# Strassen's left operands made one by one, the residual spread, and single PSUM banks in the last block

## The chip, the cores and the metric

The kernel runs on one core of a Trainium2 chip. The metric is the device time of one execution in microseconds (us), the median of three runs. The program is one launch with no arithmetic on the host.

## The reference

One layer of a transformer block on a sequence of 512 tokens with width 2048, all in float32. The part that the change touches is the second half:

```python
x = layer_norm(alpha * x + gate1 * mix, ln1_g, ln1_b)
u2 = x * (1.0 + scale2) + shift2
h = jnp.square(jax.nn.relu(u2 @ w_mlp_up)) @ w_mlp_down      # 2048 -> 8192 -> 2048
x = layer_norm(alpha * x + gate2 * h, ln2_g, ln2_b)
```

Before it come two attention branches and their projections, which the change leaves as they are.

## The kernel before

Every float32 operand of a large product is split into a rounded high part and a low part (`whi` and `wlo` for weights): ScalarE copies the high part out, VectorE subtracts it from the original to get the low part. One product is then three matmuls into the same PSUM bank (lines 206 to 208). Line 208 of the up projection, and line 207 of the down products, are the ones that read `wlo`.

The 8192 hidden columns are worked in 16 blocks of 512. Blocks 0 to 12 use Strassen's seven products for the down projection. For block `fb` the kernel merges two lists of steps:

- the up projection of block `fb`: eight steps, called U0 to U7 below. A step loads two 128-row weight tiles, splits them, and does 24 matmuls of 512 columns. After U7 the relu (ScalarE) and the multiplication (VectorE) write the tiles `rA` and `rB`, first `rA` from the first PSUM pair, then `rB`.
- the down products of block `fb - 1`: fourteen steps, the seven products in the order 1, 5, 2, 7, 6, 3, 4 for each of two column halves. They are called P1, P5 and so on, with a dash (P1') in the second half. A step loads or combines weight tiles (`draw`, five buffers), splits them, does 12 matmuls of 512 columns into a PSUM pair and adds that to an accumulator (line 1177; in the first Strassen block ScalarE copies it instead, line 1175).

Each product needs a left operand (`sh`, `sl`), made from `rA` and `rB` by `s_ops`: a split on ScalarE and VectorE for each of the seven, and four more VectorE operations of the same size that combine quarters (lines 1109, 1110, 1114, 1118). In the kernel before, an object `Ahead` makes them: as soon as the last up step has been written down, every left operand whose buffer the previous block has used for the last time is made, and the rest follow as their buffers come free. In program order they stand ahead of P3', P4' and of U0 of the next block.

The order of instructions on each engine isn't the program order: a planner walks through the program with its own cost estimates and gives each engine, whenever it is free, the earliest instruction in program order that is ready by then. Each engine then runs its list strictly in that order. So program order is a priority.

`residual(cb)` (lines 1058 to 1070) scales and shifts one 512-column block of the residual by `ln1_g` and `ln1_b`: two loads on POOL's queue, two multiplications on ScalarE, four VectorE operations of 1024 elements, two stores to DRAM (`x_d`) on POOL's queue. All four run beside the second half of the up projection of block 0, `mlp_up(0, 1)`. After it the PSUM pool is closed and a new one with pairs of banks (tags `u` and `d`) is opened.

The last block (lines 1308 to 1339) goes by four token tiles t and four column groups g: 12 matmuls into half of a PSUM pair (`ed`), an add into the residual, statistics. After the four groups the tile is normalised: ScalarE scales, then a multiplication and an addition by POOL (t = 0, 1, and g = 0 of t = 2) or VectorE (the other groups of t = 2); t = 3 is finished by VectorE alone, with two fused operations for each group.

Of the kernel before, what the change touches and what calls it, by code (L numbers as in the profile page):

```python
# [84 lines left out]
def tile_block(  # L85
# [182 lines left out]
    def merge(*lists, lo=0.0, hi=1.0):  # L268
        order = []
        for n, l in enumerate(lists):  # L270
            b0, b1 = (lo, hi) if n else (0.0, 1.0)
            order += [(b0 + (i + 0.5) / len(l) * (b1 - b0), n, i) for i in range(len(l))]
        order.sort()
        for _, n, i in order:
            lists[n][i]()
# [551 lines left out]
    def advance(force=False):  # L827
        nonlocal step_no
        step_no += 1
        while pend and (pend[0][0] <= step_no or force):  # L830
            pend.pop(0)[1]()
# [196 lines left out]
    def mlp_up(fb, half=None, r=None):  # L1028
        r = [] if r is None else r
        ts_ = slice(0, S) if half is None else slice(half * 256, half * 256 + 256)  # L1030
        hold = {}

        def mk():
            hold["d"] = [pair(f"u{fb}_{j}", "u") for j in range(2)]
            return [d[:, j] for d in hold["d"] for j in range(2)]

        def done(banks):
            if not r:
                r.extend(hp.tile([P, 2, S], F32, name=n, tag=n, bufs=1) for n in ("rA", "rB"))
            if half is None:  # L1040
                for rt, d in zip(r, hold["d"]):
                    nc.scalar.activation(rt, d, AF.Relu)
                    nc.vector.tensor_mul(rt, rt, d)
            else:
                for j in range(4):
                    rt = r[j // 2][:, j % 2, ts_]
                    nc.scalar.activation(rt, banks[j][:, ts_], AF.Relu)
                    nc.vector.tensor_mul(rt, rt, banks[j][:, ts_])  # L1048

        return r, group_fm(  # L1050
            w_mlp_up[0], fb * 512, 512, u2, all_k, f"u{fb}_{half}", done, ps, ts_, wload2,
            mk if half is None else None,
        )
# [3 lines left out]

    def residual(cb):
        cs = slice(cb * 512, (cb + 1) * 512)
        g1t = opp["p"].tile([P, 512], F32, name=f"g1t{cb}", tag="g1t", bufs=2)  # L1060
        b1t = opp["p"].tile([P, 512], F32, name=f"b1t{cb}", tag="b1t", bufs=2)
        nc.gpsimd.dma_start(g1t, ln1_g[0:1, cs].broadcast_to([P, 512]))
        nc.gpsimd.dma_start(b1t, ln1_b[0:1, cs].broadcast_to([P, 512]))
        nc.scalar.mul(g1t, g1t, ALPHA)
        nc.scalar.mul(b1t, b1t, ALPHA)
        for h_ in range(2):
            rc = res2[h_][:, :, cs]
            nc.vector.tensor_mul(rc, rc, g1t.unsqueeze(1).broadcast_to([P, 2, 512]))
            nc.vector.tensor_add(rc, rc, b1t.unsqueeze(1).broadcast_to([P, 2, 512]))
            nc.gpsimd.dma_start(x_d[h_][cb].rearrange("p (t c) -> p t c", t=2), rc)  # L1070
# [1 line left out]

    r_new, steps = mlp_up(0, 0)
    merge(steps, u2_steps(1), lo=0.1, hi=0.9)
    merge(mlp_up(0, 1, r_new)[1], [lambda c_=c_: residual(c_) for c_ in range(4)])
    st_o.close()
    st_ps.close()
    psd["p"], st_ps = pool("ps3", space=PSUM)
    ctx.callback(st_ps.close)

# [2 lines left out]

    sp, st_sp = pool("strassen")
    ORD = (1, 5, 2, 7, 6, 3, 4)

    def s_tiles(i):
# [29 lines left out]
        return [(1, lambda: split(1, a11)), (5, m5), (2, lambda: split(2, a12)), (7, lambda: split(7, a11)),  # L1121
                (6, m6), (3, m3), (4, lambda: split(4, a22))]

    class Ahead:
        def __init__(self):
            self.todo, self.free = [], set(ORD)

        def advance(self):
            while self.todo and self.todo[0][0] in self.free:
                i, fn = self.todo.pop(0)  # L1130
                self.free.discard(i)
                fn()

    ahead = Ahead()

    def strassen(fb, ops):
        st = {}

        def step(cg, i):
            def raw(j, k):  # L1140
                return wraw(
                    w_mlp_down[0][fb * 512 + (j - 1) * 256 : fb * 512 + j * 256, (k - 1) * 1024 + cg * 512 : (k - 1) * 1024 + cg * 512 + 512],
                    sp, "draw", 5,
                )

            if i == 1:
                w = st["b11"] = raw(1, 1)
            elif i == 5:
                st["b12"] = raw(1, 2)
                w = st["b11"]  # L1150
                nc.vector.tensor_sub(w, st["b12"], w)
            elif i == 2:
                w = st["b21"] = raw(2, 1)
            elif i == 7:
                st["b22"] = raw(2, 2)
                w = st["b12"]
                nc.vector.tensor_sub(w, st["b22"], w)
            elif i == 6:
                w = st["b11"]
                nc.vector.tensor_sub(w, st["b22"], w)  # L1160
            elif i == 3:
                w = st["b22"]
            else:
                w = st["b11"]
                nc.vector.tensor_sub(w, w, st["b21"])
            wh, wl = parts(w)
            db = pair(f"p{fb}_{cg}_{i}", "d")
            sh, sl = ops[i]
            for t in range(2):
                ts_ = slice(t * P, (t + 1) * P)  # L1170
                for k in range(2):
                    mm3(db[:, t], sh[:, k, ts_], sl[:, k, ts_], wh[k], wl[k], k == 0, k == 1)
            ac = acc[i][:, :, cg * 512 : cg * 512 + 512]
            if fb == 0:
                nc.scalar.copy(ac, db)
            else:
                nc.vector.tensor_add(ac, ac, db)  # L1177
            if cg == 1:
                ahead.free.add(i)
            ahead.advance()  # L1180

        return [lambda cg=cg, i=i: step(cg, i) for cg in range(2) for i in ORD]

    ops = {}
    ahead.todo = s_ops(r_new, ops)
    ahead.advance()
    for fb in range(1, NSB + 1):
        r_new, steps = mlp_up(fb)
        nxt = {}

        def begin(r_new=r_new, nxt=nxt, fb=fb):
            if fb < NSB:
                ahead.todo = s_ops(r_new, nxt)
                ahead.advance()

        last_up = steps.pop()

        def last_step(last_up=last_up, begin=begin):
            last_up()
            begin()  # L1200

        steps.append(last_step)
        merge(steps, strassen(fb - 1, ops), lo=0.1, hi=1.1)
        ops = nxt


    def load_g2b(tiles):
# [97 lines left out]
    lw, st_lw = pool("lastw", side="right")  # L1305
    merge(down_steps(NFB - 2, prev), [lambda g=g, k0=k0: last_w(lw, g, k0) for g in range(4) for k0 in (0, 2)], lo=0.2, hi=1.0)
    prev = cur
    for t in range(NT):
        st = ep.tile([P, 4, 6], F32, name=f"st2_{t}")
        rt = res[t]  # L1310
        for g in range(4):
            cs = slice(g * 512, (g + 1) * 512)
            if g % 2 == 0:
                ed = pair(f"e{t}_{g}", "du"[g // 2])
            bk = ed[:, g % 2]
            for k in range(4):
                wh, wl = lwt[g, k // 2 * 2]
                ts_ = slice(t * P, (t + 1) * P)
                mm3(bk, prev[k][0][:, ts_], prev[k][1][:, ts_], wh[k % 2], wl[k % 2], k == 0, k == 3)
            nc.vector.tensor_add(rt[:, cs], rt[:, cs], bk)  # L1320
            nc.vector.bn_stats(st[:, g, :], rt[:, cs])
        mv = ep.tile([P, 2], F32, name=f"mv2_{t}")
        nc.vector.bn_aggr(mv, st)
        ve = ep.tile([P, 1], F32, name=f"ve2_{t}")
        nc.vector.tensor_scalar_add(ve, mv[:, 1:2], LN_EPS)
        y = rstd(ep, ve, 1, f"n2{t}")
        nm = ep.tile([P, 1], F32, name=f"nm2_{t}")
        nc.vector.scalar_tensor_tensor(nm, mv[:, 0:1], -1.0, y, ALU.mult, ALU.mult)
        for g in range(4):
            cs = slice(g * 512, (g + 1) * 512)  # L1330
            if t < NT - 1:
                nc.scalar.activation(rt[:, cs], rt[:, cs], AF.Identity, bias=nm, scale=y)
                eng = nc.gpsimd if t < 2 or g == 0 else nc.vector
                eng.tensor_mul(rt[:, cs], rt[:, cs], g2t[:, cs])
                eng.tensor_add(rt[:, cs], rt[:, cs], b2t[:, cs])
            else:
                nc.vector.scalar_tensor_tensor(rt[:, cs], rt[:, cs], mv[:, 0:1], g2t[:, cs], ALU.subtract, ALU.mult)
                nc.vector.scalar_tensor_tensor(rt[:, cs], rt[:, cs], y, b2t[:, cs], ALU.mult, ALU.add)
            nc.sync.dma_start(out[0][t * P : (t + 1) * P, cs], rt[:, cs])
    st_lw.close()  # L1340
    st_e.close()
    st_dp.close()
# [28 lines left out]
```

## Time and profile before

| | |
|---|---|
| median of three runs | 2807.77 us (2805.59 to 2807.94) |
| the profiled execution | 2807.5 us, of which its span 2805.7 us |
| mean granted TensorE clock | 0.98 of full speed |
| busy: TensorE, VectorE, ScalarE, POOL | 96%, 68%, 37%, 7% of the span |

The numbered groups further down quote the trace. A row of a timeline has the start in us from the span's start, the length in us, the engine (PE is TensorE, DVE VectorE, ACT ScalarE), the line, the operation and what it writes and reads; in brackets stands the idle time just before it, with what ended it. A row of a waits view has the total in us, the number of waits and the longest. Rows that overlap are normal on PE, where matmuls are pipelined: the distance from one start to the next is what one costs.

### The profile page before, as it was taken

Reading aid. Unit: us, or ns where it says so; the run is one execution under the profiler, and the core shown is the slowest. Engines: PE = TensorE matmul, PEld = TensorE weight load, DVE = VectorE, ACT = ScalarE, POOL = GpSimd, SP = SyncE. Lnnn points to the kernel's source line nnn. Section 1 sums busy time; section 2 is a strip of 40 time slices with the busy share of each in tenths; the row PEclk is TensorE's granted clock in tenths of the full one; section 3 lists DMA queues with packets and bytes.
Section 4 is the critical chain, followed back from the end, with each engine's and each line's share of the span. In section 5 each row is a group of like instructions: output and inputs, shape, how many; then the busy total and the mean of one; then the engine's idle time right before and its main releaser. Section 6 shows DMA issues by size and latency. Waiting matters only on the chain.

```text
span 2805.7 us, 33125 instructions
## 1 busy us (share of the span) xinstructions
PE 2699.3 (96%) x12456; PEld 2233.2 (80%) x12456; DVE 1915.9 (68%) x2761; ACT 1030.9 (37%) x1668; POOL 189.3 (7%) x236
## 2 busy tenths in 40 slices
PE   7999999999999999999999999999999999999997
PEld 6888998888777777787888778777877778778885
DVE  6984347655588877537866776776666776679575
ACT  4433242222377642224644332333323333333231
POOL 0212000000122211100000000000000000000003
PEclk9999999999999999999999999999999999999998
DMA  8773339877511157535653233322323233235331
GB/s 295 263 237 91 98 120 310 277 262 234 194 50 42 61 182 250 194 128 177 194 196 112 76 105 98 98 93 88 105 90 98 90 98 106 83 105 188 98 128 60
DMA packets 217100, 404.94 MB, mean 144 GB/s; under 512 B 18334, under 2 KB 45124, under 8 KB 216172
## 3 DMA queue, kind: packets, MB, share of 16 engines
q1 hardware_dynamic: 207824, 370.61, 40.6%
q0 software_dynamic: 8928, 32.14, 3.4%
q8 instruction: 98, 1.61, 0.2%
q14 instruction: 62, 0.51, 0.1%
q10 hardware_dynamic: 188, 0.07, 0.0%
HBM read 385.94 MB, written 16.83 MB: 144 GB/s over the span
## 4 chain that ended last, share of the span: by engine, by line
PE 50%; DVE 8%; DMA 2%; issue 1%; ACT 1%; POOL 0%; DVEq 0%; ACTq 0%; POOLq 0%
PE u L208 8%; PE u L206 7%; PE u L207 7%; PE p L208 5%; PE p L207 5%; PE p L206 5%; PE o L207 2%; PE o L208 2%; PE o L206 2%; DVE sl L1106 1%; DVE res L1177 1%; DVE wlo L1013 1%; PE bb L208 1%; PE bb L206 1%; PE bb L207 1%
## 5 line engine op out<-in xcount | busy, mean ns | idle before, releaser
L199 ACT CAST whi<-raw 128x512 fp32r<-128x512 f32 (+4 forms) x456 | 269.9, 597 | 565.7 <-PE g L207 204.6
L208 PE MATMUL u<-u2h,wlo 128*128 128x512 f32 (+1 forms) x1088 | 423.1, 392 | 51.5 <-DVE wlo L1013 51.4
L200 DVE TENSOR_TENSOR wlo<-raw,whi 128x512 fp32r<-128x512 f32 (+4 forms) x456 | 301.8, 674 | 244.2 <-ACT whi L199 242.8
L206 PE MATMUL u<-u2h,whi 128*128 128x512 f32 (+1 forms) x1088 | 420.3, 387 | 2.2 <-DVE rB L1048 2.2
L207 PE MATMUL u<-u2l,whi 128*128 128x512 f32 (+1 forms) x1088 | 419.5, 386 | 0.0
L348 DVE SCALAR_TENSOR_TENSOR acc<-araw,csil,acc 128x512 f32<-128x512 f32 (+1 forms) x382 | 279.2, 749 | 83.9 <-DMA araw<-in_w_ada_dram 78.9
L1012 ACT CAST whi<-draw 128x1024 fp32r<-128x1024 f32 x182 | 191.9, 1055 | 382.6 <-PE p L208 235.1
L1013 DVE TENSOR_TENSOR wlo<-raw,whi 128x1024 fp32r<-128x1024 f32 x152 | 185.5, 1221 | 186.4 <-ACT whi L1012 186.2
L1012 ACT CAST whi<-raw 128x1024 fp32r<-128x1024 f32 x152 | 159.7, 1051 | 393.4 <-PE u L207 319.5
L1013 DVE TENSOR_TENSOR wlo<-draw,whi 128x1024 fp32r<-128x1024 f32 x182 | 221.9, 1220 | 100.2 <-ACT whi L1012 100.2
L208 PEld LDWEIGHTS u<-u2h,wlo 128*128 128x128 f32 x1088 | 212.9, 196 | 96.2 <-DVE wlo L1013 56.5
L207 PE MATMUL p<-wlo,sh 128*128 128x512 f32 x728 | 283.2, 389 | 0.0
L208 PE MATMUL p<-whi,sl 128*128 128x512 f32 x728 | 283.2, 389 | 0.0
L206 PE MATMUL p<-whi,sh 128*128 128x512 f32 x728 | 283.2, 389 | 0.0
L206 PEld LDWEIGHTS u<-u2h,whi 128*128 128x128 f32 x1088 | 212.4, 195 | 41.6 <-DVE rB L1048 2.4
L207 PEld LDWEIGHTS u<-u2l,whi 128*128 128x128 f32 x1088 | 211.2, 194 | 40.1
L206 PE MATMUL g<-uh,whi 128*128 128x512 f32 x512 | 201.3, 393 | 0.0
L208 PE MATMUL g<-uh,wlo 128*128 128x512 f32 x512 | 200.3, 391 | 0.0
L207 PE MATMUL g<-ul,whi 128*128 128x512 f32 x512 | 200.1, 391 | 0.0
L207 PEld LDWEIGHTS p<-wlo,sh 128*128 128x128 f32 x728 | 136.7, 188 | 28.5
L206 PEld LDWEIGHTS p<-whi,sh 128*128 128x128 f32 x728 | 136.7, 188 | 28.4
L208 PEld LDWEIGHTS p<-whi,sl 128*128 128x128 f32 x728 | 136.6, 188 | 28.2
(379 smaller groups left out, 4891.4 us busy)
## 6 DMA issues: line engine op xcount, KB each, us to landing
araw<-in_w_ada_dram SPq DMA_DIRECT2D x192, 512.0 KB, 5.0
raw<-in_w_mlp_up_dram SPq DMA_DIRECT2D x136, 512.0 KB, 3.7
draw<-in_w_mlp_down_dram SPq DMA_DIRECT2D x104, 512.0 KB, 3.4
raw<-in_w_in_dram SPq DMA_DIRECT2D x96, 512.0 KB, 5.1
raw<-in_w_out_dram SPq DMA_DIRECT2D x48, 512.0 KB, 3.5
raw<-in_w_mlp_down_dram SPq DMA_DIRECT2D x24, 512.0 KB, 3.4
gate_d<-sg POOLq DMA_DIRECT2D x32, 256.0 KB, 5.8
raw<-in_w_branch_fox_dram SPq DMA_DIRECT2D x16, 512.0 KB, 4.9
```

Of the source, the lines that this page charges most:

```text
L199: nc.scalar.copy(hi, rv[:, k])
L200: nc.vector.tensor_sub(lo, rv[:, k], f(hi))
L206: nc.tensor.matmul(o, ah, bh, start=start, stop=False)
L207: nc.tensor.matmul(o, ah, bl, start=False, stop=False)
L208: nc.tensor.matmul(o, al, bh, start=False, stop=stop)
L348: nc.vector.scalar_tensor_tensor(ac, rv[:, kk, :], ck_, ac, ALU.mult, ALU.add)
L1012: nc.scalar.copy(hi, raw)
L1013: nc.vector.tensor_sub(lo, raw, f(hi))
L1106: nc.vector.tensor_sub(lo, a, f(hi))
L1177: nc.vector.tensor_add(ac, ac, db)
```

## The change

- `residual` takes one tile of the `draw` buffers for both vectors instead of two of its own, and ScalarE scales both in one instruction. Residuals 0 and 2 stay beside `mlp_up(0, 1)`, at 0.55 and 1.05 of its length; residuals 1 and 3 move into the first Strassen block, between P6 and P3 and between P3 and P4. The pool of the Strassen tiles is opened earlier for that.
- `Ahead` goes. At the start of each block the left operand of product 1 is made, that of product 5 after U0, and each product step then makes one more, two products ahead. The fourteen product steps and the one for operand 5 are spread over the same length as before, so U0 and U1 now stand together ahead of P1.
- Before the last block the PSUM pool is closed and one with eight single banks is opened.
- For t = 2, POOL finishes groups 0 to 2. Group 3 stays with VectorE and is put off until the statistics of group 2 of t = 3 have been written down.

```diff
     def residual(cb):
         cs = slice(cb * 512, (cb + 1) * 512)
-        g1t = opp["p"].tile([P, 512], F32, name=f"g1t{cb}", tag="g1t", bufs=2)
-        b1t = opp["p"].tile([P, 512], F32, name=f"b1t{cb}", tag="b1t", bufs=2)
+        gb = sp.tile([P, 2, 512], F32, name="draw", tag="draw", bufs=5)
+        g1t, b1t = gb[:, 0], gb[:, 1]
         nc.gpsimd.dma_start(g1t, ln1_g[0:1, cs].broadcast_to([P, 512]))
         nc.gpsimd.dma_start(b1t, ln1_b[0:1, cs].broadcast_to([P, 512]))
-        nc.scalar.mul(g1t, g1t, ALPHA)
-        nc.scalar.mul(b1t, b1t, ALPHA)
+        nc.scalar.mul(gb, gb, ALPHA)
...
-    merge(mlp_up(0, 1, r_new)[1], [lambda c_=c_: residual(c_) for c_ in range(4)])
     st_o.close()
+    sp, st_sp = pool("strassen")
+    merge(mlp_up(0, 1, r_new)[1], [lambda c_=c_: residual(c_) for c_ in (0, 2)], lo=0.3, hi=1.3)
     st_ps.close()
     psd["p"], st_ps = pool("ps3", space=PSUM)
...
-            if cg == 1:
-                ahead.free.add(i)
-            ahead.advance()
+
+            if lefts:
+                lefts.pop(0)[1]()
...
     for fb in range(1, NSB + 1):
+        ops = {}
+        lefts = s_ops(r_new, ops)
         r_new, steps = mlp_up(fb)
-        nxt = {}
-
-        def begin(r_new=r_new, nxt=nxt, fb=fb):
-            if fb < NSB:
-                ahead.todo = s_ops(r_new, nxt)
-                ahead.advance()
...
-        merge(steps, strassen(fb - 1, ops), lo=0.1, hi=1.1)
-        ops = nxt
+        first, second = lefts.pop(0)[1], lefts.pop(0)[1]
+        down = strassen(fb - 1, ops, lefts)
+        if fb == 1:
+            down.insert(6, lambda: residual(3))
+            down.insert(5, lambda: residual(1))
+        first()
+        down.insert(0, second)
+        merge(steps, down, lo=0.1, hi=1.1)
...
+    st_ps.close()
+    ps, st_ps = pool("ps4", space=PSUM)
+    ctx.callback(st_ps.close)
+    late = []
     for t in range(NT):
...
-            if g % 2 == 0:
-                ed = pair(f"e{t}_{g}", "du"[g // 2])
-            bk = ed[:, g % 2]
+            bk = bank(f"e{t}_{g}", "e", 8, ps)
...
             nc.vector.bn_stats(st[:, g, :], rt[:, cs])
+            if g == 2:
+                while late:
+                    late.pop()()
...
-                eng = nc.gpsimd if t < 2 or g == 0 else nc.vector
-                eng.tensor_mul(rt[:, cs], rt[:, cs], g2t[:, cs])
-                eng.tensor_add(rt[:, cs], rt[:, cs], b2t[:, cs])
+
+                def finish(eng, t=t, rt=rt, cs=cs):
+                    eng.tensor_mul(rt[:, cs], rt[:, cs], g2t[:, cs])
+                    eng.tensor_add(rt[:, cs], rt[:, cs], b2t[:, cs])
+                    nc.sync.dma_start(out[0][t * P : (t + 1) * P, cs], rt[:, cs])
+
+                if t < 2 or g < 3:
+                    finish(nc.gpsimd)
+                else:
+                    late.append(lambda finish=finish: finish(nc.vector))
```

## Rows read from the trace of the kernel before

**Rows 1.** the page of the profile: span, and busy time of each engine

```profile
span 2805.7 us, 33125 instructions
...
PE 2699.3 (96%) x12456; PEld 2233.2 (80%) x12456; DVE 1915.9 (68%) x2761; ACT 1030.9 (37%) x1668; POOL 189.3 (7%) x236
```

**Rows 2.** waits of TensorE over the whole span: total us, times, longest

```profile
PE u L208 <- DVE wlo L1013: 51.4, 12, 4.5
```

**Rows 3.** waits of TensorE, blocks from 1590 to 2485 us

```profile
PE u L208 <- DVE wlo L1013: 49.8, 11, 4.5
```

**Rows 4.** timeline of TensorE, one block's end, and the last such end

```profile
1574.76 0.39 PE L208 MATMUL p<-whi,sl 128*128 128x512 f32 x1
...
1589.04 0.39 PE L208 MATMUL p<-whi,sl 128*128 128x512 f32 x1
...
1590.17 0.39 PE L206 MATMUL p<-whi,sh 128*128 128x512 f32 x1
1595.09 0.79 PE L208 MATMUL u<-u2h,wlo 128*128 128x512 f32 x1 [4.53 <-DVE wlo L1013]
...
1597.38 0.63 PE L206 MATMUL u<-u2h,whi 128*128 128x512 f32 x1
...
1599.09 0.62 PE L207 MATMUL u<-u2l,whi 128*128 128x512 f32 x1
...
2482.04 0.80 PE L208 MATMUL u<-u2h,wlo 128*128 128x512 f32 x1 [4.53 <-DVE wlo L1013]
```

**Rows 5.** timeline of VectorE at the same block's end

```profile
1584.27 0.69 DVE L1106 TENSOR_TENSOR sl<-rA,sh 128x512 fp32r<-128x512 f32 x1 [0.69 <-ACT sh L1105]
...
1585.61 1.21 DVE L1043 TENSOR_TENSOR rB<-rB,u 128x1024 f32<-128x1024 f32 x1
...
1593.22 0.68 DVE L1106 TENSOR_TENSOR sl<-rB,sh 128x512 fp32r<-128x512 f32 x1
1593.82 1.22 DVE L1013 TENSOR_TENSOR wlo<-raw,whi 128x1024 fp32r<-128x1024 f32 x1
1594.95 0.68 DVE L1106 TENSOR_TENSOR sl<-rB,sh 128x512 fp32r<-128x512 f32 x1
```

**Rows 6.** windows: stretch and its us; busy PE, PEld, DVE, ACT, POOL; clock; DMA; GB/s

```profile
1436.00:1500.00 64.00, 64.00 (x284) 52.99 (x284) 29.10 (x24) 28.62 (x30) 0.00 (x0) 1.00 0.34 105
1396.00:1430.00 34.00, 30.21 (x218) 28.45 (x218) 30.96 (x38) 15.91 (x25) 5.59 (x9) 0.95 0.92 318
1600.00:1678.00 78.00, 78.00 (x345) 64.56 (x344) 50.72 (x46) 26.41 (x28) 0.00 (x0) 1.00 0.31 100
1590.00:1600.00 10.00, 5.47 (x15) 4.00 (x14) 9.97 (x12) 2.04 (x3) 0.00 (x0) 0.66 0.28 68
2556.00:2566.00 10.00, 10.00 (x46) 8.29 (x45) 10.00 (x10) 4.90 (x5) 2.13 (x4) 1.00 0.86 256
```

**Rows 7.** timeline of TensorE, end of the second half of block 0

```profile
1413.14 0.39 PE L208 MATMUL u<-u2h,wlo 128*128 128x256 f32 x1 [1.56 <-DVE wlo L1013]
...
1424.29 0.50 PE L206 MATMUL u<-u2h,whi 128*128 128x512 f32 x1 [2.15 <-DVE rB L1048]
```

**Rows 8.** DMA issues by kind: count, size, median us to landing

```profile
x_d<-res POOLq DMA_DIRECT2D x8, 512.0 KB, 5.1
...
b1t<-in_ln_b_dram POOLq DMA_DIRECT2D x4, 256.0 KB, 5.9
```

**Rows 9.** timeline of TensorE, the last block's end

```profile
2782.58 0.39 PE L208 MATMUL e<-lwh,hl 128*128 128x512 f32 x1
2788.56 0.79 PE L206 MATMUL e<-lwh,hh 128*128 128x512 f32 x1 [5.59 <-DVE res L1320]
...
2793.42 0.63 PE L208 MATMUL e<-lwh,hl 128*128 128x512 f32 x1
```

**Rows 10.** line 1334 on POOL and on VectorE: ns min/median/max

```profile
L1334 POOL TENSOR_TENSOR res<-res,g2t x9: 1288/1294/1305, 2757.9 to 2781.4; 128x512 f32<-128x512 f32 x9
...
L1334 DVE TENSOR_TENSOR res<-res,g2t x3: 678/679/1184, 2782.0 to 2785.4; 128x512 f32<-128x512 f32 x3
```

More of the change, by code (lines that the diff above doesn't have):

```diff
@@ L1074, in tile_block @@
     merge(steps, u2_steps(1), lo=0.1, hi=0.9)
-    merge(mlp_up(0, 1, r_new)[1], [lambda c_=c_: residual(c_) for c_ in range(4)])
     st_o.close()
+    sp, st_sp = pool("strassen")
+    merge(mlp_up(0, 1, r_new)[1], [lambda c_=c_: residual(c_) for c_ in (0, 2)], lo=0.3, hi=1.3)
     st_ps.close()
     psd["p"], st_ps = pool("ps3", space=PSUM)
-    ctx.callback(st_ps.close)
-    sp, st_sp = pool("strassen")
     ORD = (1, 5, 2, 7, 6, 3, 4)
@@ L1122, in s_ops, with strassen @@
                 (6, m6), (3, m3), (4, lambda: split(4, a22))]
[L1124 to L1136, printed above, removed]
+    def strassen(fb, ops, lefts):
         st = {}
@@ L1177, in step @@
                 nc.vector.tensor_add(ac, ac, db)
-            if cg == 1:
-                ahead.free.add(i)
-            ahead.advance()
+            if lefts:
+                lefts.pop(0)[1]()
         return [lambda cg=cg, i=i: step(cg, i) for cg in range(2) for i in ORD]
-    ops = {}
-    ahead.todo = s_ops(r_new, ops)
-    ahead.advance()
     for fb in range(1, NSB + 1):
+        ops = {}
+        lefts = s_ops(r_new, ops)
         r_new, steps = mlp_up(fb)
-        nxt = {}
-        def begin(r_new=r_new, nxt=nxt, fb=fb):
-            if fb < NSB:
-                ahead.todo = s_ops(r_new, nxt)
[L1194 to L1202, printed above, removed]
-        merge(steps, strassen(fb - 1, ops), lo=0.1, hi=1.1)
-        ops = nxt
+        first, second = lefts.pop(0)[1], lefts.pop(0)[1]
[6 more added lines that the diff above has]
+        merge(steps, down, lo=0.1, hi=1.1)
     def load_g2b(tiles):
@@ L1338, in tile_block @@
                 nc.vector.scalar_tensor_tensor(rt[:, cs], rt[:, cs], y, b2t[:, cs], ALU.mult, ALU.add)
-            nc.sync.dma_start(out[0][t * P : (t + 1) * P, cs], rt[:, cs])
+                nc.sync.dma_start(out[0][t * P : (t + 1) * P, cs], rt[:, cs])
     st_lw.close()
```

## The prediction

> **What bounds the kernel now.** I read the page first: TensorE is busy for 2699.3 of 2805.7 us, so the change can only earn what is left, and VectorE, at 68%, is no bound as an average [rows 1]. Next, the waits of TensorE: one line holds nearly all of the wait behind the attention part, 51.4 us in 12 waits for a weight's low part, `wlo` [rows 2], of which 49.8 us in 11 equal waits lie between 1590 and 2485 us [rows 3]. That is one at the end of each Strassen block from the third on.
>
> Third, the timeline of one such end. At full clock matmuls start every 0.2267 us: 63 of these steps lie between 1574.76 and 1589.04 [rows 4]. By 1590.17 TensorE has done what it can without U0's `wlo`; the next matmul, line 208 of U0, comes at 1595.09, so 4.92 − 0.23 = 4.69 us are lost. Then matmuls start every 0.43 us (1597.38 to 1599.09, four steps), because the granted clock is at its half level: the window from 1590 to 1600 shows 0.66 on average, and the 78 us behind it show 1.00 [rows 6]. TensorE stood idle just before that fall.
>
> A block has 8 x 24 + 14 x 12 = 360 matmuls, 81.6 us at full pace. From the first of the eleven waits to the last (1595.09 to 2482.04, ten blocks) a block takes 88.70 us [rows 4]. So one end costs 88.695 − 81.61 = 7.08 us, wait and half clock together, and eleven cost 77.9 us.
>
> Fourth, why `wlo` is late. On VectorE a full-size operation (1024 elements) costs 1.14 us from start to start and a half-size one 0.60 (1593.82 to 1594.95, and 1593.22 to 1593.82) [rows 5]. Between the first left operand (1584.27) and U0's `wlo` (1593.82) stand ten half-size operations of the left operands, the multiplication of `rB` and two accumulator adds: 6.0 + 3 x 1.14 = 9.4 of 9.55 us. U0's weights are behind the left operands because those stand earlier in program order, though the last of these operands, for P6, is needed only three up steps and four products after U0's start, 27 us later.
>
> **Part 1, left operands one by one.** Nothing is removed: eleven half-size VectorE operations and seven ScalarE copies a block as before. They move behind U0 in priority; only the split for product 1 stays ahead. By the rows, nine of the ten half-size operations leave the path: 9 x 0.60 = 5.4 us, so `wlo` starts at 1593.82 − 5.4 = 1588.4 and ends at 1589.6. The second of the two adds can't start before P4' ends at about 1589.5, so `wlo` is likelier to go ahead of it and end about a microsecond earlier. U0's first matmul is free to start at 1589.27, its third at 1589.72. So `wlo` comes in time by 0.1 to 1.3 us, and the wait goes whole; with no wait I expect no fall of the clock, as in the full stretches of [rows 6].
>
> What is late next? I checked three things. (a) VectorE in the block: 50.7 of 78 us busy without the left operands that the end takes [rows 6], so 5.4 us fit. The densest stretch, one up step and two products, is 10.9 us of TensorE; it holds three `wlo`, two adds and one weight difference (6 x 1.14 = 6.8) and at most four half-size operations (2.4), 9.2 together. (b) The left operand itself: from the end of a product to the start of the one two further on lie one product and one up step, 2.7 + 5.4 = 8.2 us. In the worst written order the operand waits for that product's add (1.14), a combination (0.60), a ScalarE copy (0.6) and a low part (0.60), 2.9 us. (c) U0 and U1 back to back: U1 has the weight buffers that P3' frees, 8.2 us ahead of its need. A boundary that is packed with other work is there to compare: at the end of the Strassen stage, 2556 to 2566 us, VectorE is busy for 10.00 of 10.00 us and so is TensorE [rows 6]; a full VectorE does no harm if the order is right.
>
> Value taken: 77.9 us. Bounds: no more, since nothing else is lost there; and as little as 0 if the planner keeps the order.
>
> **Part 2, residual.** Around the end of block 0 TensorE waits 1.56 us for `wlo` and 2.15 us for the last multiplication of `rB`, which frees a bank for the new PSUM pool [rows 7]; the clock of 0.95 over 34 us is another 0.05 x 34 = 1.7 us [rows 6]. VectorE is busy for 31.0 of these 34 us, and moving two residuals takes 2 x 4 x 1.14 = 9.1 us away, with the left operands beyond the second behind U0 as well. I let the 1.56 us go, keep the 2.15 us (the banks still wait for the same multiplication) with most of the half clock, and take a gain of 2.2 us. In the first Strassen block, which ScalarE's copies relieve, VectorE is busy for 29.1 of 64 us [rows 6], and 9.1 us fit. What can bite is ScalarE: its scaling waits for two loads on POOL's queue, 5.9 us to landing, behind two stores of the residual before [rows 8], and `whi` for the next steps stands behind it; weights are split 5.4 us ahead, so a wait of that length costs up to 2 us, twice. The two `draw` buffers come out of five, of which weights hold four. Bounds: −4 to +5.4.
>
> **Part 3, the last block.** The last 12 matmuls wait 5.59 us for an add, since their bank shares a tile with group 2's, and the add stands on VectorE behind t = 2's finishing. They start 2788.56 − 2782.58 = 5.98 us behind the one before, 5.75 more than the pace, and go at 0.44 a step (11 steps in 4.86 us instead of 2.49) [rows 9]: 8.1 us. With a bank of its own group 3 waits for nothing. What comes next is VectorE: two put-off operations ahead of the last add, then the fused ones. POOL now has six operations instead of two for t = 2, 1.29 us each from 2781.4 on, so until about 2789, beside the two and the first four fused ones. The row shows what that does: the same VectorE operation takes 0.68 us as median and 1.18 at most while POOL works [rows 10]. Six operations at 0.5 us each are 3.0 us, none at best; I take 1.5 and a gain of 6.6 us.
>
> The Trainium skill (SBUF — State Buffer, section "SBUF: two separate sides") calls the pair of ports that VectorE and GpSimd share an exclusive lock, held for a whole instruction, which an operation with two SBUF inputs must get. By that rule the tail would earn 4.2 instead of 6.6 us (rival D); the row's 0.5 us agrees in kind and is smaller.
>
> The new PSUM pool is the other price: the last block's first bank may have to wait for the last add of the block before, a full-size one. I take zero, with −1.1 as the lower bound; nothing is to be gained, since the waits view names no other wait of the last block.
>
> **The sum**, against the profiled execution's own 2807.5 us: 77.9 + 6.6 + 2.2 = 86.7, so 2720.8, 2721 rounded. The median shown is 0.3 us above that execution, which changes nothing.
>
> **The rivals.**
> A. Half a wait stays. If both adds and the first combination get ahead of U0's `wlo` (2 x 1.14 + 0.60 behind the multiplication of `rB` at 1586.8, with P4' ending at 1589.5), it ends near 1591.9, and TensorE waits up to 2.2 us; taking 1.7, it is 11 x 1.7 = 19 us, 2740, and with a fall of the clock as now (2.2 us each) 2764. For it: the planner has its own cost estimates. Against: `wlo` is ready before P4' ends.
> B. The change doesn't do what it says: the planner, who only looks at what is ready, still fills VectorE with the left operands first. Then parts 2 and 3 alone count: 2807.5 − 8.8 = 2799. Against: U0 now has priority, and its `whi` needs only U7's buffer.
> C. Slower: operands come late. If VectorE's list holds a stretch's six full-size operations (6.8 us) ahead of an operand's 2.9, it misses its product by 9.7 − 8.2 = 1.5 us; five operands a block in 13 blocks are 98 us, so 2807.5 − 86.7 + 98 = 2819. It decides from 86.7 / 65 = 1.3 us for each operand on. For it: an operand now has one chance, and the list is in order. Against: the 27 us of idle VectorE in 78.
> D. The tail is held by POOL: if each of the six VectorE operations waits for what is left of a POOL instruction, half of 1.29 us on average [rows 10], that is 0.65 each and 3.9 together, the tail earns 8.1 − 3.9 = 4.2, and the time is 2807.5 − 77.9 − 2.2 − 4.2 = 2723. Against: the row's median shows most of them undisturbed. The skill's rule quoted in part 3 is this rival.
>
> **How the numbers follow.** Forecast 0.73, A 0.13, B 0.05, C 0.05, D 0.04. The forecast's own range is 2716 to 2730: below, all losses named (77.9, 5.4 and 8.1) gone; above, part 2 at its lower bound of −4 and 3 us less from the tail. With D, which lies in it, and the half of A without a fall of the clock, 2713 to 2741 holds some 0.83; the last 3 us below are for the scatter of the runs, which lie 2.4 us apart. A measurement of this kernel tells 0.2%, 5.6 us, from no change: the forecast, A, B and D are all faster by more (0.95 together); of C's 0.05 I count 0.01 as no change and 0.04 as slower.
>
> **What would show it.** Right: blocks of 81.6 to 82 us, no wait of TensorE on line 1013 above a microsecond, a granted clock of 1.00 from 1430 us to the end, and U0's `wlo` on VectorE ahead of all but the first left operand. For the tail: the last 12 matmuls at once behind the others, with VectorE operations of over 1 us beside POOL's. Wrong: waits for `sl` (line 1106), a wait for a `draw` load or for the scaling of the residual in the first Strassen block, or equal waits at each block's end as now.

## The result, and the profile after

The changed kernel takes 2725.67 us (median of 4 runs, 2723.03 to 2725.87) beside 2807.16 (2805.59 to 2807.94): ratio 0.9708, interval 0.9691 to 0.9725. A second time, beside other kernels, it gave the same ratio (0.9708, 0.9695 to 0.9722). Forecast were 2721, in a range of 2713 to 2741: the measured time lies in the range, 4.7 us above the value.

The page of the changed kernel: TensorE has lost 30 us of busy time with the same 12456 matmuls, since fewer of them run at the half clock (mean granted clock 0.99, where it was 0.98).

```profile
span 2724.0 us, 33092 instructions
...
PE 2669.7 (98%) x12456; PEld 2216.8 (81%) x12456; DVE 1910.9 (70%) x2757; ACT 1029.3 (38%) x1664; POOL 193.6 (7%) x240
```

The waits of TensorE from 1366 to 2800 us (total us, times, longest). The first line answers to [rows 2]: of the 51.4 us, 2.8 are left. For the stretch of [rows 3] the view no longer has any line.

```profile
...
PE u L208 <- DVE wlo L1013: 2.8, 2, 2.3
PE d L207 <- DVE wlo L1013: 2.4, 3, 1.3
PE u L206 <- DVE rB L1048: 2.2, 1, 2.2
...
```

The timeline of VectorE at the block's end that [rows 5] show. Between the first left operand and U0's `wlo` stand one combination and the multiplication of `rB`; both adds (line 1163) and U1's `wlo` come behind. The end lies 2.60 us later on this run's clock than in [rows 5] (1586.87 for 1584.27), so times are counted from the first left operand: `wlo` starts 2.47 us behind it, where it was 9.55.

```profile
1586.87 0.69 DVE L1104 TENSOR_TENSOR sl<-rA,sh 128x512 fp32r<-128x512 f32 x1 [0.69 <-ACT sh L1103]
1587.60 0.69 DVE L1107 TENSOR_TENSOR rA<-rA 128x512 f32<-128x512 f32 x1
1588.21 1.21 DVE L1043 TENSOR_TENSOR rB<-rB,u 128x1024 f32<-128x1024 f32 x1
1589.34 1.22 DVE L1013 TENSOR_TENSOR wlo<-raw,whi 128x1024 fp32r<-128x1024 f32 x1
1590.47 1.22 DVE L1163 TENSOR_TENSOR res<-res,p 128x1024 f32<-128x1024 f32 x1
...
1593.34 1.22 DVE L1013 TENSOR_TENSOR wlo<-raw,whi 128x1024 fp32r<-128x1024 f32 x1
```

The timeline of TensorE there, beside [rows 4]: P4' runs into U0 at the pace of 0.2267 us. U0's first matmul that reads `wlo` starts at 1592.32, and `wlo` was written by 1589.34 + 1.22 = 1590.56, so 1.76 us are in hand.

```profile
1591.64 0.39 PE L208 MATMUL p<-whi,sl 128*128 128x512 f32 x1
1591.87 0.39 PE L206 MATMUL u<-u2h,whi 128*128 128x512 f32 x1
1592.09 0.39 PE L207 MATMUL u<-u2l,whi 128*128 128x512 f32 x1
1592.32 0.39 PE L208 MATMUL u<-u2h,wlo 128*128 128x512 f32 x1
```

Two windows of [rows 6] again (stretch and its us; busy PE, PEld, DVE, ACT, POOL; clock; DMA; GB/s). At the block's end the clock is at 1.00 where it was 0.66; VectorE is as full as before. At the end of block 0 it is still 0.95.

```profile
1396.00:1430.00 34.00, 31.36 (x228) 29.70 (x227) 28.97 (x35) 15.88 (x24) 3.86 (x6) 0.95 0.88 281
1590.00:1600.00 10.00, 10.00 (x45) 8.28 (x45) 10.00 (x12) 4.72 (x7) 0.00 (x0) 1.00 0.37 105
```

Where the parts of the change act is read in three stretches of TensorE's timeline: from block 0's first up step to the last block's first down step (`d`), from there to the end, and the part ahead, which the change leaves alone: TensorE's instructions are the same in the same order up to there. For the changed kernel they are bounded by 1368.42 and 2533.00 us, the starts of the first matmuls into `u` and into `d`.

| us, profiled runs | ahead | up step to `d` | `d` to end | span |
|---|---|---|---|---|
| before | 1366.06 | 1242.42 | 197.23 | 2805.7 |
| before, second profile | 1369.12 | 1243.56 | 197.94 | 2810.6 |
| changed | 1368.42 | 1164.58 | 190.97 | 2724.0 |
| changed, second profile | 1371.63 | 1164.98 | 190.59 | 2727.2 |
| left operands alone | 1365.13 | 1161.70 | 197.64 | 2724.5 |
| last block alone | 1371.52 | 1239.25 | 190.49 | 2801.3 |
| residual as before | 1368.25 | 1161.49 | 191.06 | 2720.8 |
| the same, second profile | 1368.58 | 1160.12 | 190.79 | 2719.5 |

The part ahead takes 1365 to 1372 us from run to run, in all fourteen profiles of this study, so an edit of a few microseconds can't be read from one span. The stretches behind repeat better, but not perfectly. Up to `d` the kernel with the last block alone has the program of the kernel before, with the same instructions in the same order, and took 1239.25 us where that took 1242.42 and 1243.56: a scatter of 4.3 us, of which some 0.6 us lie at the block ends and the rest in block 0. The changed program has three more profiles up to `d`, from the experiments that alter only the last block: 1164.18, 1163.06 and 1163.56 us, so it scatters by 1.9 us. From `d` to the end the scatter is under 1 us.

### The profile page after: what moved, and what is told of

The parts are those of the page before. It is cut to its first block, busy times and chain, and to the rows that moved or that the text cites. A ratio compares the mean times of both kernels' runs of the same rounds, so it can differ in the third digit from the quotient of the medians.

```text
span 2724.0 us, 33092 instructions
## 1 busy us (share of the span) xinstructions
PE 2669.7 (98%) x12456; PEld 2216.8 (81%) x12456; DVE 1910.9 (70%) x2757; ACT 1029.3 (38%) x1664; POOL 193.6 (7%) x240
## 4 chain that ended last, share of the span: by engine, by line
PE 50%; DVE 3%; issue 3%; DMA 3%; ACT 1%; POOL 0%; DVEq 0%; ACTq 0%; POOLq 0%; SPq 0%
PE u L208 7%; PE u L206 7%; PE u L207 7%; PE p L206 6%; PE p L208 6%; PE p L207 6%; PE o L207 2%; PE o L208 2%; PE o L206 2%; DMA raw<-in_w_mlp_down_dram 1%; DMA araw<-in_w_ada_dram 1%; PE d L207 1%; DMA draw<-in_ln_b_dram 1%; PE d L208 1%; PE d L206 1%
## 5 line engine op out<-in xcount | busy, mean ns | idle before, releaser
L206 PE MATMUL u<-u2h,whi 128*128 128x512 f32 (+1 forms) x1088 | 412.3, 379 | 2.2 <-DVE rB L1048 2.2
L208 PE MATMUL u<-u2h,wlo 128*128 128x512 f32 (+1 forms) x1088 | 411.2, 378 | 2.8 <-DVE wlo L1013 2.8
L207 PE MATMUL u<-u2l,whi 128*128 128x512 f32 (+1 forms) x1088 | 411.3, 378 | 0.0
L208 PEld LDWEIGHTS u<-u2h,wlo 128*128 128x128 f32 x1088 | 205.8, 189 | 41.1 <-DVE wlo L1013 3.4
L206 PEld LDWEIGHTS u<-u2h,whi 128*128 128x128 f32 x1088 | 206.1, 189 | 39.8 <-DVE rB L1048 2.4
```

Source lines behind the costliest of these rows:

```text
L206: nc.tensor.matmul(o, ah, bh, start=start, stop=False)
L207: nc.tensor.matmul(o, ah, bl, start=False, stop=False)
L208: nc.tensor.matmul(o, al, bh, start=False, stop=stop)
```

## The experiments

The theory at the start was the prediction's: the block's end is gone because U0's `wlo` no longer stands behind the left operands; the last block earns by its banks and its finishing together; the residual is worth little. Rivals: another edit than the one named earns the block's end, the number of operands ahead doesn't matter, the spread residual pays.

**Parts alone.** The left operands alone (the kernel before, with the `strassen` loop of the changed one):

```
-    ahead.todo = s_ops(r_new, ops)
-    ahead.advance()
...
+        lefts = s_ops(r_new, ops)
...
+        first, second = lefts.pop(0)[1], lefts.pop(0)[1]
+        down = strassen(fb - 1, ops, lefts)
+        first()
+        down.insert(0, second)
```

> The kernel before with part 1 alone: left operands one by one, two products ahead; residual and last block as before. Theory (the waits at the block ends come from the left operands' place ahead of U0's weights on VectorE): the eleven block ends go whole, 77.9 us, with 0 to 2.5 us more at the end of block 0, where fewer operands stand ahead: 2727 to 2730 us, blocks of 81.6 us. Rival 1 (the waits need the new PSUM pools or the moved residual to go): above 2790. Rival 2 (half a wait stays without the other parts): about 2745.

Measured: 2730.94 us (ratio 0.9728, 0.971 to 0.9746), a microsecond above the expected range; the profiled run 2726.24. Its waits of TensorE show the tail's wait untouched and none at the blocks' ends; a block takes 81.60 us:

```profile
PE e L206 <- DVE res L1296: 5.6, 1, 5.6
PE u L206 <- DVE rB L1048: 2.0, 1, 2.0
...
PE u L208 <- DVE wlo L1013: 1.0, 1, 1.0
...
```

The last block alone (single banks in a new pool, new finishing):

```
-            if g % 2 == 0:
-                ed = pair(f"e{t}_{g}", "du"[g // 2])
-            bk = ed[:, g % 2]
+            bk = bank(f"e{t}_{g}", "e", 8, ps)
...
+                if t < 2 or g < 3:
+                    finish(nc.gpsimd)
+                else:
+                    late.append(lambda finish=finish: finish(nc.vector))
```

> The kernel before with part 3 alone: single banks in the last block, POOL finishes groups 0 to 2 of t = 2, group 3 is put off. Theory (the last 12 matmuls wait for no add any more, and VectorE is 1 us slower behind them beside POOL): 6 to 6.5 us less, 2801 us, with the block ends' waits as before. Rival (POOL's six operations hold VectorE up by as much as the matmuls gain): within 2 us of before, 2805 to 2808.

Measured: 2802.24 us (0.9977, 0.9967 to 0.9986), some 6.5 us less by the ratio. The waits keep the 49.8 us of [rows 3] and have no line for `e`. The two parts touch different waits and add up.

The residual put back, with the two other parts kept, measured twice:

```
-    merge(mlp_up(0, 1, r_new)[1], [lambda c_=c_: residual(c_) for c_ in (0, 2)], lo=0.3, hi=1.3)
+    merge(mlp_up(0, 1, r_new)[1], [lambda c_=c_: residual(c_) for c_ in range(4)])
...
-            down.insert(6, lambda: residual(3))
-            down.insert(5, lambda: residual(1))
```

> The changed kernel with all four residuals beside the second half of block 0, in their own buffers, as before. Theory (the spread removes the short wait in block 0 and puts another into the first Strassen block, where ScalarE waits for a load on POOL's queue): within 1.5 us of the changed kernel, 2724 to 2727; the 2.3 us wait at about 1459 us gone, a wait of 1.5 us or so at about 1413 us back. Rival (the spread earns what it takes from VectorE): 3 to 5 us slower than the changed kernel, 2729 to 2731.

> The changed kernel with part 2 undone, again, in more rounds beside the changed kernel itself. If the spread residual is a net loss as the first look says (1352.5 us from the first up step on, against 1355.6 for the changed kernel), this one is 2 to 3 us below the changed kernel in the median and again near 1352.5 in that stretch. Rival (the difference is scatter, since the unchanged part ahead takes 1365 to 1371 us from run to run): the two stretches come within 1 us of each other.

> The changed kernel itself, again, beside the two others. If its stretches belong to the program and not to the run, the first up step of block 0 to the end takes 1355 to 1356.5 us again, with the wait for wlo near the end of the first Strassen block (some 2 us) and one fall of the granted clock at the end of block 0. Rival (these are scatter): the stretch comes out up to 3 us shorter, without that wait.

Measured: 2722.79 us (0.9697, 0.9681 to 0.9713), and 2722.20 (0.9697, 0.9683 to 0.9711) beside 2726.03 for the changed kernel. The intervals overlap, but the profiles don't: from the first up step to `d` 1161.49 and 1160.12, and 1161.70 with the left operands alone, against 1163.06 to 1164.98 in the five profiles of the changed program. The difference of the means is 3.0 us, and it sits in one place: the first Strassen block takes 81.60 us in all three with the old residual and 83.67 to 85.84 in all five with the spread one, 3.1 us more in the mean. The expectation of 1.5 at most was too low. In the median the kernel with the old residual lies below the changed kernel both times. Its waits (second profile) and the window at block 0's end, where the clock is now 1.00:

```profile
...
PE u L206 <- DVE rB L1048: 0.9, 1, 0.9
...
PE u L208 <- DVE wlo L1013: 0.6, 1, 0.6
...
```

```profile
1396.00:1430.00 34.00, 31.77 (x236) 29.97 (x235) 32.60 (x39) 17.33 (x29) 6.48 (x10) 1.00 0.93 322
```

**How many operands ahead of U0.** The first operand ahead of U0, and all the others right behind it:

```
-        down.insert(0, second)
+        def rest(second=second, lefts=lefts):
+            second()
+            while lefts:
+                lefts.pop(0)[1]()
+        down.insert(0, rest)
```

> The changed kernel, but all left operands from the second on are made at once behind U0, not one by one. Theory (VectorE's list decides, wherever the operands stand): U1's weights now stand behind seven half-size operations and two adds and come about 1.0 us late at each of eleven block ends: 2737 us, with a wait of TensorE of about 1 us on U1; if the granted clock falls at each of them as well, 2.2 us more each, 2761. Rival (only the place ahead of U0 matters, the spreading is nothing): 2725 to 2727 and no wait.

Measured: 2735.01 us (0.9739, 0.9724 to 0.9755). The wait comes back, one step later (for U1's `wlo`), but small: in the blocks from 1590 to 2485 us

```profile
PE u L208 <- DVE wlo L1013: 2.8, 11, 0.3
```

and a block takes 82.15 us instead of 81.60, so 11 x 0.55 = 6 us; the rest lies in the first Strassen block (86.56 us, with a wait of 2.1 us for `p`, line 207). The sign was right, and the price of an end half of what I expected.

Five operands ahead of U0:

```
-        down.insert(0, second)
+        second()
+        for _ in range(3):
+            lefts.pop(0)[1]()
+        down.insert(0, lambda: None)
```

> The changed kernel, with five left operands (products 1, 5, 2, 7, 6) made ahead of U0 in program order again, all else as changed. Theory (the place in program order is the cause): U0's weights stand behind four more half-size operations and both adds, and TensorE waits about 3.6 us for them at each of eleven block ends, for line 1013; with the half clock behind such a wait (2.2 us) that is 64 us more, 2785 to 2792; should the clock not fall, 40 us, 2765. Rival (the change helped because U1 now stands ahead of P1, or by the other parts): 2725 to 2730 and no wait.

Measured: 2766.10 us (0.985, 0.9834 to 0.9866). The timeline of VectorE at the same end:

```profile
1589.40 0.68 DVE L1104 TENSOR_TENSOR sl<-rA,sh 128x512 fp32r<-128x512 f32 x1
1590.00 1.21 DVE L1163 TENSOR_TENSOR res<-res,p 128x1024 f32<-128x1024 f32 x1
1591.13 0.68 DVE L1108 TENSOR_TENSOR rA<-rA,rB 128x512 f32<-128x512 f32 x1
1591.73 0.68 DVE L1104 TENSOR_TENSOR sl<-rB,sh 128x512 fp32r<-128x512 f32 x1
1592.33 1.21 DVE L1163 TENSOR_TENSOR res<-res,p 128x1024 f32<-128x1024 f32 x1
1593.46 0.68 DVE L1104 TENSOR_TENSOR sl<-rA,sh 128x512 fp32r<-128x512 f32 x1
1594.07 1.22 DVE L1013 TENSOR_TENSOR wlo<-raw,whi 128x1024 fp32r<-128x1024 f32 x1
```

U0's `wlo` starts at 1594.07 instead of 1589.34 (the two ends lie 0.06 us apart). Of the 4.67 us, four half-size operations account for 2.4; the other 2.3 are the two adds, which have become ready meanwhile. Both adds ahead of `wlo` is what rival A supposed. TensorE pays, in its timeline:

```profile
1594.03 0.50 PE L206 MATMUL p<-whi,sh 128*128 128x512 f32 x1 [1.05 <-ACT whi L1012]
1595.34 0.50 PE L208 MATMUL u<-u2h,wlo 128*128 128x512 f32 x1 [0.81 <-DVE wlo L1013]
```

The first of the two waits is for the `whi` of P1, of which one matmul stands ahead of U0's line 208. It adds nothing of its own: `wlo` is written only by 1594.07 + 1.22 = 1595.29, and the matmul that reads it starts at 1595.34. So it is the place of U0's `wlo` among the left operands that decides: this kernel and the changed one differ only in how early the left operands are made.

**The tail's two halves.** Single banks with the finishing of before:

```
-                if t < 2 or g < 3:
-                    finish(nc.gpsimd)
-                else:
-                    late.append(lambda finish=finish: finish(nc.vector))
+                eng = nc.gpsimd if t < 2 or g == 0 else nc.vector
...
```

> The changed kernel with single banks in the last block, but the finishing of t = 2 as before (POOL group 0, VectorE groups 1 to 3, nothing put off). Theory (the bank frees TensorE, the finishing frees VectorE): the last 12 matmuls still follow at once, but the last add stands behind four more VectorE operations: from the last matmul's start to the end 15 to 16 us instead of 13.2. Rival (the single banks carry all of it): 12.3 to 13.2 us.

Measured, in one run: from the last matmul to the end 14.95 us, just under the expected 15 to 16, where the changed kernel takes 13.21 and the one before 12.30. The last 12 matmuls come without a wait, but the last add stands behind six finishing operations (from 2708.40 on) and starts at 2716.01.

The finishing alone, with the pairs of banks and the old PSUM pool put back:

```
-            bk = bank(f"e{t}_{g}", "e", 8, ps)
+            if g % 2 == 0:
+                ed = pair(f"e{t}_{g}", "du"[g // 2])
+            bk = ed[:, g % 2]
```

> The changed kernel with the last block in shared pairs as before, but with the new finishing. Theory (group 3's matmuls wait for group 2's add, which now stands behind two VectorE operations instead of six): a wait of TensorE of 2.5 to 3.5 us ahead of the last 12 matmuls instead of 5.6, the first matmuls of the block early again beside the step before; from the first down step of block 13 to the end 2 to 4.5 us more than the changed kernel. Rival (the finishing alone carries it, the pairs cost nothing): no wait ahead of the last 12 matmuls above 1 us.

Measured, in one run: 193.04 us from `d` to the end, 2.1 more than the changed kernel, with this wait of TensorE (somewhat below the 2.5 to 3.5 expected):

```profile
PE e L206 <- DVE res L1299: 2.2, 1, 2.2
```

Of the wait of 5.59 us [rows 9] the finishing takes 3.4 by itself, and the banks the last 2.2. In time the two halves are worth about the same: from `d` to the end the kernel before takes 197.6 us, the banks alone 192.45, the finishing alone 193.04 and both 190.8. Neither is enough alone.

What POOL costs VectorE there (left out: POOL's multiplications and additions for groups 0 to 2 of t = 2):

```
+                    if t < 2 or eng is nc.vector:
+                        eng.tensor_mul(rt[:, cs], rt[:, cs], g2t[:, cs])
+                        eng.tensor_add(rt[:, cs], rt[:, cs], b2t[:, cs])
```

> The changed kernel with POOL's multiplication and addition left out for groups 0 to 2 of t = 2 (so those outputs lack gain and bias). Theory (VectorE's operations wait for POOL's at the end): from the last matmul's start to the end 12.1 to 12.4 us instead of 13.2, and no VectorE operation of line 1317, 1318 or 1326 above 0.8 us. Rival (the tail is longer because two put-off operations stand ahead of the last add): 13 us or more.

Measured, in one run: 12.06 us from the last matmul to the end, where the changed kernel has 13.21. The timelines of VectorE, first of the changed kernel, then of this one (its lines are one further down), with the three operations that run beside POOL:

```profile
2707.88 1.15 DVE L1317 TENSOR_TENSOR res<-res,g2t 128x512 f32<-128x512 f32 x1 [1.09 <-ACT res L1314]
...
2709.55 1.17 DVE L1318 TENSOR_TENSOR res<-res,b2t 128x512 f32<-128x512 f32 x1
...
2713.77 1.09 DVE L1326 SCALAR_TENSOR_TENSOR res<-res,mv,g2t 128x512 f32<-128x512 f32 x1
```

```profile
2708.36 0.69 DVE L1318 TENSOR_TENSOR res<-res,g2t 128x512 f32<-128x512 f32 x1 [1.09 <-ACT res L1314]
...
2709.57 0.68 DVE L1319 TENSOR_TENSOR res<-res,b2t 128x512 f32<-128x512 f32 x1
...
2713.44 0.74 DVE L1327 SCALAR_TENSOR_TENSOR res<-res,mv,g2t 128x512 f32<-128x512 f32 x1
```

0.46 + 0.49 + 0.35 = 1.30 us, of which 1.15 show in the tail. The adds between them, which read a PSUM bank and one SBUF operand, take 0.67 to 0.69 in both. So of these operations only those with two SBUF operands were longer beside POOL. This fits the rule of the Trainium skill that the prediction weighed (SBUF — State Buffer, section "SBUF: two separate sides"): an operation with two SBUF inputs has to get the ports that VectorE shares with GpSimd (POOL).

**Why the spread residual costs.** In the changed kernel TensorE waits near the end of the first Strassen block; its timeline, and those of ScalarE, of POOL's queue and of VectorE ahead of that:

```profile
1458.91 0.50 PE L208 MATMUL u<-u2h,wlo 128*128 128x512 f32 x1 [2.33 <-DVE wlo L1013]
```

```profile
1453.13 1.06 ACT L1064 ACTIVATE draw<-draw 128x1024 f32<-128x1024 f32 x1 [5.88 <-DMA draw<-in_ln_b_dram]
1454.09 1.03 ACT L1012 CAST whi<-raw 128x1024 fp32r<-128x1024 f32 x1
```

```profile
1443.82 0.69 POOL L1069 DMA_DIRECT2D x_d<-res  x1 [2.73 <-DVE res L1068]
1444.45 0.62 POOL L1062 DMA_DIRECT2D draw<-in_ln_g_dram  x1
1444.99 0.63 POOL L1063 DMA_DIRECT2D draw<-in_ln_b_dram  x1
```

```profile
1454.22 2.36 DVE L1067 TENSOR_TENSOR res<-res,draw 128x1024 f32<-128x1024 f32 x2 [5.72 <-ACT draw L1064]
...
1457.63 1.22 DVE L1013 TENSOR_TENSOR wlo<-raw,whi 128x1024 fp32r<-128x1024 f32 x1
```

The loads are issued behind a store that waits for VectorE. ScalarE can start 8.1 us after the issue of the second one (1444.99 to 1453.13); ScalarE and VectorE stand still for it, the `whi` of a later step is queued behind the scaling, and its `wlo` behind two multiplications and an addition of the residual. To test whether POOL's queue is what makes them late, residuals 1 and 3 were loaded by SP:

```
+        q = nc.sync if cb % 2 else nc.gpsimd
+        q.dma_start(g1t, ln1_g[0:1, cs].broadcast_to([P, 512]))
+        q.dma_start(b1t, ln1_b[0:1, cs].broadcast_to([P, 512]))
```

> The changed kernel with the two loads of residuals 1 and 3 issued by SP instead of POOL, nothing else. In the trace of the changed kernel TensorE waits 2.3 us at 1459 us for a wlo that VectorE makes late, behind two multiplications that waited for ScalarE's scaling, which waited for these loads; POOL had issued them behind two stores of the residual before. Theory (the order on POOL's queue is what makes them late): the loads land earlier, ScalarE's idle time ahead of the scaling falls from 5.9 us to under 2, the wait at 1459 goes, and the stretch from the first up step of block 0 to the last block falls from 1164.6 to about 1161.5 to 1162.5 us, 2 to 3 us less in all. Rival (the buffer of the loads comes free late, whatever the queue): the wait and the 1164 us stay, within 0.7 us, since the issue only waits on another queue.

Measured: 2725.39 us (0.97, 0.9687 to 0.9713), no different from the changed kernel's 2726.03; the stretch 1163.39 us, between the two expectations and inside the scatter of the changed program (1163.06 to 1164.98); waits of `u` at line 208 of 1.5 us in all, 1.0 at most. The first Strassen block takes 82.91 us, less than in any of the five profiles with POOL's loads (83.67 to 85.84). ScalarE's idle time ahead of the scaling is smaller and still there:

```profile
1451.17 1.06 ACT L1065 ACTIVATE draw<-draw 128x1024 f32<-128x1024 f32 x1 [3.88 <-DMA draw<-in_ln_b_dram]
```

SP issued the second load at 1445.62 and ScalarE started 5.55 us later. That SP issued no earlier than POOL has a reason in its waits, and in VectorE's timeline:

```profile
SPq L1063 <- DVE res L1069: 17.0, 1, 17.0
```

```profile
1443.94 1.22 DVE L1069 TENSOR_TENSOR res<-res,draw 128x1024 f32<-128x1024 f32 x1
```

The first load waited for VectorE's last addition of the residual before, which reads the `draw` buffer and ends at 1445.16; SP issued it at 1445.23. In the changed kernel that addition ends at 1443.53, and POOL issued at 1444.45 and 1444.99. So with either queue the loads can't go before the buffer is free, as the rival said, and what comes behind that differs with the queue: 9.6 us from the free buffer to ScalarE's start with POOL, 6.0 with SP. In the first Strassen block that is some 1.8 of the 3.1 us, by one profile. What loads with buffers of their own would take was not tested.

**The kernel before, profiled again**, to see what belongs to a run:

> The kernel before itself, again, for a second profile. The part ahead of block 0's first up step, which the change leaves alone, took 1366.06 us in its first profile and between 1365.1 and 1371.6 in ten kernels whose TensorE program is the same up to there. Theory (that part scatters from run to run, and the change's worth has to be read behind it): from that step to the end it takes 1439.7 us again, within 1 us, and the part ahead lies anywhere between 1365 and 1372. Rival (the changed kernel delays that part, 1368.4 and 1371.6): here it comes out at 1366 again, within 0.5 us.

The part ahead came out at 1369.12, so it scatters without any change; the rest took 1441.50, 1.8 us above the first profile instead of within 1.

## Why the prediction held, step by step

Measured terms are differences of stretches: means of the two profiles of before, the two of the changed kernel, and the three that have the new left operands with the old residual. With the four further profiles of the same programs up to `d` the left operands come to 80.6 and the residual to −3.0.

| step | predicted | measured |
|---|---|---|
| left operands | 77.9 | 1242.99 − 1161.10 = 81.9 |
| residual | +2.2 | 1161.10 − 1164.78 = −3.7 |
| last block | 6.6 | 197.59 − 190.78 = 6.8 |
| sum | 86.7 | 85.0 |
| part ahead | 0 | 1367.59 − 1370.03 = −2.4 |

- **Left operands: mechanism and size right.** Blocks went from 88.70 to 81.60 us, so 7.10 each, 78 over eleven, by the order that the prediction described. Counted from the first left operand, `wlo` was predicted at 1588.4 − 1584.27 = 4.1 us and started at 2.47: one combination more than I counted stayed ahead of it (0.6), and both adds fell behind it (2.3), as the prediction held likelier for one of them. U0's first matmul starts 5.0 us behind that operand in both kernels, so 1.76 us are in hand where 0.1 to 1.3 were expected. The 4 us beyond 77.9 (2.7 with all profiles) lie around the end of block 0. What earns them is open: there the waits and the clock scatter in the kernel before itself, where the wait of [rows 7] for `wlo` is 0.3 us in the second profile and 0.9 with the clock at 1.00 in the kernel with the last block alone. With the new left operands and the old residual it is 0.4 to 1.0 us.
- **Residual: the step that failed.** "I let the 1.56 us go ... and take a gain of 2.2 us" had the wrong sign. At block 0's end nothing clear of the scatter was gained: the wait for `rB` is 2.1 to 2.4 us in the five profiles with the spread and 0.7, 0.9 and 2.0 without, and the half clock is there in four of the five with it and in none of the three without. What I named as able to bite, ScalarE's scaling behind late loads, bit once, in the first Strassen block, which takes 83.67 to 85.84 us instead of 81.60; in the second profile of the changed kernel the clock also fell behind that wait (0.97 from 1430 to 1500 us). That wait was one of the named signs of being wrong. The lower bound of −4 held it. I had the mechanism and gave it no weight in the value taken, because I counted VectorE's free time in that block and not the order of the queue in front of it, nor when the shared buffer comes free.
- **Last block: size right, one price missed.** The last 12 matmuls follow at once. From the first down matmul to the last `e` TensorE takes 177.6 us instead of 185.4, so 7.8 against 8.1 predicted. The new PSUM pool, priced at zero, costs half a microsecond. In the kernel before, three matmuls of the last block run early, while a down step's `wlo` is still being made; with the new pool they can't, and TensorE waits there. The finishing alone, which keeps the old pool, has the early matmuls and not the wait. Before, then changed:

```profile
2735.69 0.39 PE L206 MATMUL e<-lwh,hh 128*128 128x512 f32 x1
...
2736.38 0.48 PE L207 MATMUL d<-wlo,hh 128*128 128x512 f32 x1
```

```profile
2662.34 0.50 PE L207 MATMUL d<-wlo,hh 128*128 128x512 f32 x1 [0.54 <-DVE wlo L1013]
```

POOL takes back 1.0 to 1.2 us, against 1.5, which was half of six slowed operations at 0.5: there were three, of 0.35 to 0.49.
- **Rivals.** A's order appears with five operands ahead, not in the changed kernel. B and C are refuted by blocks of 81.60 us and by the absence of any wait for `sl`. D took 0.35 to 0.49 for three operations instead of 0.65 for six. The argument against D misread its row: "the row's median shows most of them undisturbed" [rows 10], but the two undisturbed operations began when POOL had nothing left to do in that kernel (its last operation ends at 2784.36):

```profile
2782.76 1.60 POOL L1335 TENSOR_TENSOR res<-res,b2t 128x512 f32<-128x512 f32 x1
```

```profile
2784.84 1.28 DVE L1334 TENSOR_TENSOR res<-res,g2t 128x512 f32<-128x512 f32 x2
```

So D was right that such an operation beside POOL is slowed, and wrong in how many meet one. A's 2.2 us for a fall of the clock should be 2.4 by the prediction's own figures (7.08 − 4.69).
- **Luck.** The total is closer than its terms: the left operands gave 2.7 to 4.0 us more than forecast and the residual 5.2 to 5.9 less, and the two errors partly cancel.
- **The remaining 2.4 us** are the part ahead of the change. The kernel before gave 1366.06 and 1369.12, the changed one 1368.42 and 1371.63, others 1365.13 to 1371.52. Whether the change shifts it by a microsecond or two at all is open.

## What to carry to other kernels

When an engine with an ordered list is full at one place and idle elsewhere, look for which of its results is needed first there, and put operands that are needed much later behind it, one at a time: two ahead of use was enough here, five brought half of the lost time back, and all at once behind U0 made a small new one. Ahead of spreading work into a stretch where an engine has free time, follow the loads of that work through their queue, see when their buffers come free, and see what stands behind the instruction that waits for them. Price an edit of a few microseconds by the stretch that it touches, not by the span, where another part of the program scatters by more, and profile the same program more than once to learn how far that stretch scatters.

## What the hardware showed that was not expected

With five operands ahead, the eleven ends had the same two waits (1.05 and 0.81 us; TensorE busy 8.15 of 10 us), and the clock fell to the half level behind eight of them; behind three it stayed at full. Two windows of that kernel (columns as in [rows 6]):

```profile
1592.00:1602.00 10.00, 8.15 (x35) 6.21 (x34) 10.00 (x13) 4.28 (x6) 0.00 (x0) 1.00 0.37 105
1676.00:1686.00 10.00, 8.15 (x28) 6.04 (x27) 9.72 (x12) 3.61 (x6) 0.00 (x0) 0.83 0.36 105
```

Blocks take 84.0 us without the fall and 85.6 with it. Behind the eleven single 4.5 us waits of the kernel before it fell each time ([rows 4, 6] show two of them), behind the eleven of 0.3 us never. So such a halt cost its own 2.4 us and on most ends 1.6 more: less than the expectation for this kernel had it.
